# Token bases of the gate: whole tokens in pairs 3 to 6, or halves of the columns in pairs 3 to 7

## The chip, the cores and the metric

The kernel runs on one core of one Trainium2 chip, in one launch. The metric is the device time of that launch in microseconds (us). The core has a matrix engine (TensorE, PE in the profile; its weight loads are listed apart as PEld), VectorE (DVE), ScalarE (ACT), GpSimd (POOL) and SyncE (SP), which issues transfers. Each engine works through its own instructions in the order in which the built program lists them, and engines wait for each other through semaphores. Weights come from the device memory (HBM) by DMA into buffers in the on-chip memory (SBUF); matmul results land in PSUM buffers, which the program names by tags ("pt", "o", "dense", "s", two of each).

## The reference

Two transformer blocks follow each other on 512 tokens of width 1024. What concerns this change is the end of the second one: a mixture of 16 experts, each of which takes the 64 tokens with the highest affinity, and behind it a gate `g` that multiplies an embedding `e`:

```python
def expert_choice_ffn(h, w_router, w_gate, w_up, w_down):
    aff = jax.nn.softmax(jnp.einsum('bsd,de->bse', h, w_router).astype(jnp.float32), axis=-1)
    gates, idx = lax.top_k(aff.transpose(0, 2, 1), cap)          # cap = 64
    xe = h[bidx, idx]
    a = jnp.einsum('becd,edf->becf', xe, w_gate)
    b = jnp.einsum('becd,edf->becf', xe, w_up)
    ye = jnp.einsum('becf,efd->becd', jax.nn.silu(a) * b, w_down)
    return jnp.zeros_like(h).at[bidx, idx].add(ye * gates[..., None].astype(h.dtype))
...
x = x + expert_choice_ffn(rms_norm(x, norm_ffn[i]), w_router[i], w_gate[i], w_up[i], w_down[i])
g = jax.nn.sigmoid(rms_norm(x, norm_ple[i]) @ w_ple_gate[i])
e = rms_norm(p[i] @ w_ple_proj[i], norm_ple_post[i])
x = x + g * e
```

An expert has 2 x 1024 x 2048 weights in and 2048 x 1024 out, all fp32.

## The kernel before

**Pairs.** The 16 experts run as 8 pairs (`pr` 0 to 7): expert 2p sits in columns 0 to 63 of the array, expert 2p+1 in 64 to 127, so the two matmuls of a step run side by side. The weights of a pair are 48 chunks of 128 x 2048 fp32 (1.049 MB each, 50.3 MB a pair), two of them for each of 24 steps. `chunk` takes the next one and issues its transfer on SP's queue into the buffer that was used longest ago; that transfer waits until PE has read the buffer's former chunk. From pair 3 on (`RETIRE`) seven such buffers are left. A pair has four sections of four steps (`ga` is the gate projection, `ua` the up projection, two steps each; `sg` is their product on DVE, `pth` its transposes on PE, copied to `hts` by ACT), and then eight steps of the down projection `yd`, in two halves of the columns. Each half ends with `yg` and `ys` (the scaled result and its split in two parts), with its transposes `pty` copied to `yt`, and with a `spread`, which adds the rows into the token array `xt` (named `xk` in the profile): per group of 128 tokens two matmuls `po` and an addition on DVE.

**The gate.** Its product, (x after the mixture) times `w_ple_gate`, is linear before the normalisation, so it is built up while the experts run. `gate_base(t)` transposes what `xt` holds for token group t (eight transposes `ptg`, two ACT copies to the single buffer `xf`) and multiplies it by the gate's weights, both halves h of 512 columns (16 matmul instructions `pg` for each); `snap[t]` notes the pair in which that was. What later pairs add to these tokens goes another way: `gate_pair` multiplies the pair's own result by the gate's weights (`z`, 16 instructions for each half of the columns), splits it on ACT and DVE (`zs`), and scatters it (`po<-zs`, two matmuls and an addition, L1637) into the bases that exist already. Pair 7's `z` stays in PSUM and joins at the end.

**Order.** Such side work stands in the list `todo` as generators; `meanwhile(n)` takes n steps of them. `between` (L1651) is called after each of the 24 steps of a pair and takes `PACE[pr]` side steps on average; from pair 4 on (`HOLD`) their instructions stand behind the step's last expert matmul. `on_the_way` advances `route(pr + 1)` beside that: `bc` on PE, `ott`, `ix`, `at` on DVE, then the gather of the next pair's tokens `xg` by POOL's queue, and then an ACT instruction (L1485) that scales them.

Of the kernel before, what the change touches and what calls it, by code (L numbers as in the profile page):

```python
# [18 lines left out]
S = 512  # L19
# [8 lines left out]
XV = 4  # L28
ADA_N = 1
PO = 10  # L30
PACE = [1.0, 1.0, 1.0, 2.2, 2.2, 2.2, 2.2, 2.2]
ROUTE_PACE = 0.5
HOLD = 4
ADDPE = [1, 3, 5, 6]
TBK = 7
RETIRE = 3
BASE = {3: [0], 4: [1], 5: [2], 6: [3]}
E_AT = 1
ADA0 = 0
ADA_EVERY = 3  # L40
# [188 lines left out]
def _build(ctx, tc, nc, a, dbg, stop):  # L229
    V, A, T, P, SY = nc.vector, nc.scalar, nc.tensor, nc.gpsimd, nc.sync  # L230
# [25 lines left out]
    def ps(name, tag, bufs, shape=(128, 512)):  # L256
        tag = tag[1:] if tag[0] == "=" else TG[0].get(name, tag)
        return psp.tile(list(shape), FT, name=name, tag=tag, bufs=bufs)
# [25 lines left out]
    def t2k(name):  # L284
        return tmp[0].tile([128, S], FT, name=name, tag="t2k", bufs=nt2k[0])
# [23 lines left out]
    def weights(src, raw=None, p_=None, bufs=2):  # L309
        with tc.high_priority(offset=WO[0]):  # L310
            return weights_(src, raw, p_, bufs)
# [11 lines left out]
    def kview(w, k):  # L323
        return [t.rearrange("p (k c) -> p k c", k=k) for t in w]
# [764 lines left out]
    for j in range(22):  # L1089
        if j % 4 == 2 and j < 12:  # L1090
            nbs.append(na_bias(j // 4))
        wg = kview(weights(a["w_up"][2 * j]), 8)
# [6 lines left out]
        t = t2k("cv")  # L1099
# [13 lines left out]
    def g_split(kk):  # L1113
        g = [pb_.tile([128, S], FR, name="gh", tag="gh", bufs=2 * NT + 2) for _ in range(2)]
        split(gm[:, kk], g[0], g[1])
        return g

    for kk in range(22 - NT):
        w = weights(a["w_dn"][kk])
        g = g_split(kk)  # L1120
# [378 lines left out]
    todo = []  # L1499
# [21 lines left out]
    ple = {}  # L1521
# [27 lines left out]
    def halves(out, w, x_, start, stop):  # L1549

        for h in range(2):
            c_ = slice(64 * h, 64 * h + 64)
            T.matmul(out[c_], w[:, c_], x_, start=start, stop=stop)  # L1553
# [39 lines left out]
        for t in range(4):  # L1593
            V.scalar_tensor_tensor(e[t], e[t], re_[:, t:t + 1], gpost, op0=OP.mult, op1=OP.mult)

    def gate_base(t):

        xf = ple["xf"]
        for f in range(2):
            pt = ps("ptg", "pt", 2)  # L1600
            for k in range(4):
                c_ = 512 * f + 128 * k
                T.transpose(pt[:, 128 * k:128 * k + 128], xt[:, t, c_:c_ + 128], K["ident"])
            A.activation(xf[:, 4 * f:4 * f + 4], pt.rearrange("p (k c) -> p k c", k=4), AF.Copy)
        snap[t] = pairs[0]
        yield
        for h in range(2):
            pg = ps("pg", "o", 2)
            for k in range(8):
                halves(pg, xf[:, k], ple["wg"][k // 2][:, k % 2, S * h:S * h + S], k == 0, k == 7)  # L1610
                yield
            V.tensor_copy(ple["g"][t][:, S * h:S * h + S], pg)

    def gate_pair(pr, yts, ott, zl):

        zl += [ps("z", "o", 2) for _ in range(2)]
        at = [(n, y) for n, c in enumerate((4, 4) if pr < 7 else (4, 2, 2)) for y in range(c)]
        left = [list(range(8)), list(range(8))]
        while left[0] or left[1]:

            ready = [h for h in range(2) if left[h] and at[left[h][0]][0] < len(yts)]
            if ready:
                h = ready[0] if pr == 7 else max(ready, key=lambda h: (len(left[h]), -h))
                k = left[h].pop(0)
                halves(zl[h], yts[at[k][0]][:, at[k][1]], ple["wg"][k // 2][:, k % 2, S * h:S * h + S], k == 0, k == 7)
            whole[:] = [not l for l in left] if pr == 7 else whole
            yield
        if pr == 7:
            return
        zs = yy("zs")  # L1630
        for h in range(2):
            y = hl(zl[h], zs[:, h])
            yield
            for t in range(4):
                if snap.get(t, 8) <= pr:
                    g_ = ple["g"][t][:, S * h:S * h + S]
                    V.tensor_tensor(g_, g_, scatter(y, ott, t), op=OP.add)  # L1637
                    yield
# [9 lines left out]
    snap, pairs, whole = {}, [0], [False, False]  # L1648
    owed, way = [0.0], [0.0]

    def between(last):  # L1651

        owed[0] += PACE[pairs[0]]
        n = int(owed[0])
# [11 lines left out]
    for pr in range(8):  # L1666
        pairs[0] = pr
        if pr:
            while pr not in routed:
                on_the_way()  # L1670
        xe = routed[pr][0]
        if pr < 7:
            ways.append(route(pr + 1))
        if pr == RETIRE:
            ple_loads()
        if pr == E_AT:
            todo.append(embedding())
        todo += [gate_base(t) for t in BASE.get(pr, ())]
        hts, flip = None, []

        def turn():

            for sec, sg in flip:
                pt = ps("pth", "pt", 2)
                for f in range(4):
                    T.transpose(pt[:, 128 * f:128 * f + 128], sg[:, 128 * f:128 * f + 128], K["ident"])  # L1686
                A.activation(hts[:, 4 * sec:4 * sec + 4], pt.rearrange("p (f s) -> p f s", f=4), AF.Copy)  # L1687
            flip.clear()

        for sec in range(4):  # L1690
            acc_ = [ps("ga", "dense", 2), ps("ua", "s", 2)]
            for m in range(2):
                for kh in range(2):
                    wa, wb = chunk(4), chunk(4)
                    for k in range(4):
                        kk = 4 * kh + k
                        T.matmul(acc_[m][0:64], xe[:, kk, 0:64], wa[:, k], start=kk == 0, stop=kk == 7)  # L1697
                        mm = T.matmul(acc_[m][64:128], xe[:, kk, 64:128], wb[:, k], start=kk == 0, stop=kk == 7)  # L1698
                    if pr == 0 and sec == 0:
                        meanwhile(1)  # L1700
                    if m == 0 and kh == 0:
                        turn()
                    between(mm)
            if hts is None:
                hts = mp.tile([128, 16, 128], FT, name="hts", tag="hts", bufs=1)
            sg = s2k("sg")
            A.activation(sg, acc_[0], AF.Silu)  # L1707
            V.tensor_tensor(sg, sg, acc_[1], op=OP.mult)  # L1708
            flip.append((sec, sg))
        turn()  # L1710
        last = pr == 7
        if last:
            tc.keep_in_program_order(A.preload_act_table_set(LN_EXP))
        _, gs, ott = routed.pop(pr)
        ys, yts, z = yy("ys"), [], []
        if pr >= min(BASE):
            todo.append(gate_pair(pr, yts, ott, z))
        for q in range(2):
            parts = 2 if last and q else 1
            n = S // parts  # L1720
            for part in range(parts):
                yd = ps("yd", "s" if q > part else "dense", 2)[:, 0:n]
                for k in range(4 // parts):
                    wa, wb = chunk(4 * parts), chunk(4 * parts)
                    for k_ in range(4 * parts):
                        kk = 4 * parts * k + k_
                        T.matmul(yd[0:64], hts[:, kk, 0:64], wa[:, k_], start=kk == 0, stop=kk == 15)  # L1727
                        mm = T.matmul(yd[64:128], hts[:, kk, 64:128], wb[:, k_], start=kk == 0, stop=kk == 15)  # L1728
                    between(mm)
                yg = s2k("yg")[:, 0:n]  # L1730
                A.activation(yg, yd, AF.Copy, scale=gs)  # L1731
                y = hl(yg, ys[:, q, :, n * part:n * part + n])
                if pr >= min(BASE):
                    pt = ps("pty", "pt", 2)[:, 0:n]
                    for k in range(n // 128):
                        T.transpose(pt[:, 128 * k:128 * k + 128], yg[:, 128 * k:128 * k + 128], K["ident"])
                    yt = mp.tile([128, 4, 128], FT, name="yt", tag="yt", bufs=2)[:, 0:n // 128]
                    V.tensor_copy(yt, pt.rearrange("p (k c) -> p k c", c=128))  # L1738
                    yts.append(yt)
                while any(t not in snap for t in BASE.get(pr, ())):  # L1740
                    meanwhile()
                if not last:
                    todo.append(spread(y, ott, q))
                for t in range(4) if last else ():
                    x_ = xt[:, t, S * q + n * part:S * q + n * part + n]
                    V.tensor_tensor(x_, x_, scatter(y, ott, t), op=OP.add)
                    if last:
                        A.activation(s2k("sq")[:, 0:n], x_, AF.Square,
                                     accum_out=sx[:, 3 * t + q + part:3 * t + q + part + 1])
# [7 lines left out]
    for h in range(2):  # L1757
# [5 lines left out]
        for t in range(4):  # L1763
            c_, n = slice(S * h, S * h + S), 4 * h + t
            o = outs[:, S * t:S * t + S]
# [34 lines left out]
```

## Time and profile before

| | |
|---|---|
| median of 3 runs | 2080.02 us (2078.24 to 2080.1) |
| the profiled execution | 2082.14 us, of which its span is 2080.4 us |
| PE busy | 1946.9 us, 94% of the span |
| DVE, ACT, POOL busy | 770.2, 587.8, 126.8 us |
| moved by DMA | 523.2 MB, mean 251 GB/s |
| pairs 3 to 7, first expert matmul at | 1402, 1524, 1657, 1787, 1918 us; pair 7 ends at 2043 |

The mean over the span hides stages with different limits. The experts begin at 1030 us, and the stretches by pair, about 125 us each, are what this change touches. In the stretch of a pair the question is which of two is late at each step: the chunk (PE waits for DMA) or the buffer (SP waits for PE before it issues the next transfer).

### The profile page before, as it was taken

The numbers are of one execution on the slowest core, as the hardware profiler recorded it, in microseconds if no ns is written. First come the engines' busy times: TensorE is split into PE (matmuls) and PEld (weight loads), VectorE is DVE, ScalarE is ACT, GpSimd is POOL, SyncE is SP. The second block draws the span as 40 slices with busy tenths as digits, with TensorE's granted clock in tenths as the row PEclk, the third lists the DMA queues.
The fourth block names the chain that finished last, engine by engine and source line by source line (L and its number), as shares of the span: only waits on it lengthen the run. The fifth ranks groups of instructions, "written<-read, shape, count | busy, mean of one in ns | idle before, by whom it ended". The sixth has DMA issues, their size and how long they took to land.

```text
span 2080.4 us, 23393 instructions
## 1 busy us (share of the span) xinstructions
PE 1946.9 (94%) x9118; PEld 1088.8 (52%) x9118; DVE 770.2 (37%) x1665; ACT 587.8 (28%) x1138; POOL 126.8 (6%) x127
## 2 busy tenths in 40 slices
PE   7989999989999998999899978789799999999998
PEld 4667667768888887776533322223233333333333
DVE  4767767764444336675431111010011021110212
ACT  4755657643323234454111110000000000000013
POOL 1210201300100000001000000030000000000000
PEclk9999989989999999999899999999999999999999
DMA  7432313422322231224889899998999999999991
GB/s 306 122 127 73 101 51 122 143 87 100 122 93 100 97 126 50 78 77 165 327 370 419 355 421 419 420 410 360 421 393 378 394 412 378 400 391 385 398 420 48
DMA packets 94191, 523.20 MB, mean 251 GB/s; under 512 B 11405, under 2 KB 11829, under 8 KB 43136
## 3 DMA queue, kind: packets, MB, share of 16 engines
q1 hardware_dynamic: 88832, 500.47, 61.6%
q0 software_dynamic: 3904, 18.88, 2.4%
q10 hardware_dynamic: 1344, 2.35, 0.3%
q8 instruction: 72, 1.18, 0.2%
q14 instruction: 39, 0.32, 0.0%
HBM read 510.31 MB, written 4.27 MB: 247 GB/s over the span
## 4 chain that ended last, share of the span: by engine, by line
PE 75%; DMA 13%; DVE 6%; ACT 3%; issue 2%; POOL 1%; DVEq 0%; POOLq 0%; ACTq 0%; SPq 0%
PE ua L1697 6%; DMA ch<-in_w_ue_dram 6%; PE ga L1697 5%; PE ga L1698 5%; DMA ch<-in_w_de_dram 4%; PE yd L1727 4%; PE yd L1728 3%; PE z L1553 3%; PE pg L1553 2%; PE od L652 2%; PE ag L327 2%; PE ag L328 2%; PE ag L329 2%; PE av L327 2%; PE av L328 2%
## 5 line engine op out<-in xcount | busy, mean ns | idle before, releaser
L1698 PE MATMUL ua<-ch,xe 128*64 128x512 f32 x512 | 230.9, 595 | 17.3 <-DMA ch<-in_w_ue_dram 17.3
L1728 PE MATMUL yd<-ch,hts 128*64 128x512 f32 (+1 forms) x544 | 231.8, 572 | 16.0 <-DMA ch<-in_w_de_dram 16.0
L1697 PE MATMUL ga<-ch,xe 128*64 128x512 f32 x512 | 242.2, 609 | 0.0
L1698 PE MATMUL ga<-ch,xe 128*64 128x512 f32 x512 | 236.8, 607 | 5.0 <-DMA ch<-in_w_ge_dram 5.0
L1697 PE MATMUL ua<-ch,xe 128*64 128x512 f32 x512 | 232.8, 595 | 0.0
L1727 PE MATMUL yd<-ch,hts 128*64 128x512 f32 (+1 forms) x544 | 232.7, 572 | 0.0
L320 DVE TENSOR_TENSOR wlo<-pan,whi 128x1024 fp32r<-128x1024 f32 x119 | 147.8, 1242 | 160.9 <-ACT whi L317 158.7
L317 ACT ACTIVATE whi<-pan 128x1024 fp32r<-128x1024 f32 x119 | 125.8, 1057 | 201.1 <-PE ag L328 84.8
L1708 DVE TENSOR_TENSOR sg<-sg,ua 128x512 f32<-128x512 f32 x32 | 22.0, 686 | 264.6 <-PE ua L1698 264.6
L1728 PEld LDWEIGHTS yd<-ch,hts 128*64 128x64 f32 x544 | 72.0, 137 | 91.2 <-issue 59.1
L1697 PEld LDWEIGHTS ua<-ch,xe 128*64 128x64 f32 x512 | 67.3, 137 | 96.3 <-issue 94.4
L1698 PEld LDWEIGHTS ga<-ch,xe 128*64 128x64 f32 x512 | 66.7, 139 | 87.8 <-issue 77.3
L1727 PEld LDWEIGHTS yd<-ch,hts 128*64 128x64 f32 x544 | 71.3, 137 | 67.3 <-issue 65.7
L355 POOL TENSOR_TENSOR ada_a<-ada_a,adw 128x512 f32<-128x512 f32 x56 | 79.3, 1416 | 378.1 <-ACT ada_a L352 270.6
L1698 PEld LDWEIGHTS ua<-ch,xe 128*64 128x64 f32 x512 | 67.4, 137 | 63.4 <-issue 32.3
L333 DVE TENSOR_TENSOR ys<-yg,ys 128x512 fp32r<-128x512 f32 (+1 forms) x17 | 12.5, 736 | 235.9 <-ACT ys L332 235.9
L1697 PEld LDWEIGHTS ga<-ch,xe 128*64 128x64 f32 x512 | 66.3, 139 | 61.6 <-issue 60.9
L1687 ACT ACTIVATE hts<-pth 128x512 f32<-128x512 f32 x32 | 19.1, 596 | 265.1 <-PE pth L1686 265.1
L1731 ACT ACTIVATE yg<-yd,gs 128x512 f32<-128x512 f32 (+1 forms) x17 | 11.3, 662 | 291.1 <-PE yd L1728 220.2
L1553 PE MATMUL z<-ch,yt 128*64 128x512 f32 x320 | 89.0, 595 | 1.4 <-DVE yt L1738 1.3
L1707 ACT ACTIVATE sg<-ga 128x512 f32<-128x512 f32 x32 | 19.1, 597 | 224.5 <-PE ga L1698 204.2
L614 ACT ACTIVATE e<-e,m 128x256 f32<-128x256 f32 (+8 forms) x128 | 64.9, 508 | 29.1 <-DVE m L612 28.7
(902 smaller groups left out, 3732.9 us busy)
## 6 DMA issues: line engine op xcount, KB each, us to landing
ch<-in_w_de_dram SPq DMA_DIRECT2D x128, 1024.0 KB, 12.1
ch<-in_w_ue_dram SPq DMA_DIRECT2D x125, 1024.0 KB, 10.1
ch<-in_w_ge_dram SPq DMA_DIRECT2D x120, 1024.0 KB, 10.1
pan<-in_w_up_dram SPq DMA_DIRECT2D x44, 512.0 KB, 3.4
adw<-in_ada_dram SPq DMA_DIRECT2D x64, 256.0 KB, 2.7
pan<-in_w_in_dram SPq DMA_DIRECT2D x24, 512.0 KB, 3.9
pan<-in_w_dn_dram SPq DMA_DIRECT2D x22, 512.0 KB, 3.4
adr<-in_ada_dram SPq DMA_DIRECT2D x8, 1024.0 KB, 12.4
```

The lines of the kernel that those rows point to most:

```text
L317: A.activation(hi, raw, AF.Copy)
L320: eng.tensor_tensor(lo, raw, hi.bitcast(FT), op=OP.subtract)
L327: T.matmul(out, wh, xh, start=first, stop=False)
L328: T.matmul(out, wh, xl, start=False, stop=False)
L329: T.matmul(out, wl, xh, start=False, stop=last)
L355: P.tensor_tensor(ada_next[1], ada_next[1], w, op=OP.add)
L614: A.activation(e[:, :nk], e[:, :nk], AF.Exp, bias=m, scale=-1.0, accum_out=l)
L1553: T.matmul(out[c_], w[:, c_], x_, start=start, stop=stop)
L1697: T.matmul(acc_[m][0:64], xe[:, kk, 0:64], wa[:, k], start=kk == 0, stop=kk == 7)
L1698: mm = T.matmul(acc_[m][64:128], xe[:, kk, 64:128], wb[:, k], start=kk == 0, stop=kk == 7)
L1727: T.matmul(yd[0:64], hts[:, kk, 0:64], wa[:, k_], start=kk == 0, stop=kk == 15)
L1728: mm = T.matmul(yd[64:128], hts[:, kk, 64:128], wb[:, k_], start=kk == 0, stop=kk == 15)
```

## The change

`BASE` now lists pairs of token group and half of the columns. Pair 3 makes the bases of groups 0 and 1 for half 0, pair 4 those of groups 2 and 3 for half 0, pair 5 groups 0 and 1 for half 1, pair 6 group 2 and pair 7 group 3 for half 1. Each base transposes its token group anew. `gate_pair` makes and scatters `z` only for halves that have a base already, so pairs 3 and 4 make it for half 0 alone. `PACE` goes down in pairs 3 to 6.

```diff
-PACE = [1.0, 1.0, 1.0, 2.2, 2.2, 2.2, 2.2, 2.2]
+PACE = [1.0, 1.0, 1.0, 1.9, 1.9, 1.9, 2.1, 2.2]
...
-BASE = {3: [0], 4: [1], 5: [2], 6: [3]}
+
+BASE = {3: [(0, 0), (1, 0)], 4: [(2, 0), (3, 0)], 5: [(0, 1), (1, 1)], 6: [(2, 1)], 7: [(3, 1)]}
...
-    def gate_base(t):
+    def gate_base(t, h):
...
-        snap[t] = pairs[0]
-        yield
-        for h in range(2):
-            pg = ps("pg", "o", 2)
-            for k in range(8):
-                halves(pg, xf[:, k], ple["wg"][k // 2][:, k % 2, S * h:S * h + S], k == 0, k == 7)
-                yield
-            V.tensor_copy(ple["g"][t][:, S * h:S * h + S], pg)
+        snap[t, h] = pairs[0]
+        yield
+        pg = ps("pg", "o", 2)
+        for k in range(8):
+            halves(pg, xf[:, k], ple["wg"][k // 2][:, k % 2, S * h:S * h + S], k == 0, k == 7)
+            yield
+        V.tensor_copy(ple["g"][t][:, S * h:S * h + S], pg)
...
-        zl += [ps("z", "o", 2) for _ in range(2)]
+        hs = [h for h in range(2) if any(c[1] == h for p_, l in BASE.items() if p_ <= pr for c in l)]
+        zl += [ps("z", "o", 2) for _ in hs]
...
-        left = [list(range(8)), list(range(8))]
+        left = [list(range(8)) if h in hs else [] for h in range(2)]
...
-        for h in range(2):
+        for h in hs:
...
-                if snap.get(t, 8) <= pr:
+                if snap.get((t, h), 8) <= pr:
...
-        todo += [gate_base(t) for t in BASE.get(pr, ())]
+        todo += [gate_base(*c) for c in BASE.get(pr, ())]
```

The diff doesn't show what this moves. Line numbers are one higher behind the change. The built programs have the same instructions in the same order on POOL and SP; PE, DVE and ACT differ from pair 3 on. Instructions counted by pair, from the pair's first expert matmul to the next pair's (an instruction `z` or `pg` covers one half of the array, 64x512; `po` counts matmuls of scatters, 128x512):

| | z | pg | ptg | po |
|---|---|---|---|---|
| pair 3, before / after | 16 / 8 | 15 / 16 | 0 / 8 | 0 / 0 |
| pair 4 | 32 / 16 | 32 / 32 | 8 / 16 | 20 / 20 |
| pair 5 | 32 / 22 | 32 / 32 | 8 / 16 | 24 / 24 |
| pair 6 | 32 / 34 | 32 / 16 | 8 / 8 | 28 / 28 |
| pair 7, up to its first `po<-ys` of its own | 16 / 16 | 0 / 16 | 0 / 8 | 32 / 30 |

Three places, word for word. First ACT at the head of pair 4, before and after (`yg`, `ys`: the end of pair 3; `sg`: the first section; `xg`: the gathered tokens, which waits for the gather; `zs`: the split of pair 3's `z`; `hts`: the first section's transposes).

```order
L1731 ACTIVATE yg<-yd,gs 128x512
L332 ACTIVATE ys<-yg 128x512
L1707 ACTIVATE sg<-ga 128x512
L1485 ACTIVATE xg<-xg 128x1024
L332 ACTIVATE zs<-z 128x512 x2
L1687 ACTIVATE hts<-pth 128x512
```

```order
L1732 ACTIVATE yg<-yd,gs 128x512
L333 ACTIVATE ys<-yg 128x512
L1708 ACTIVATE sg<-ga 128x512
L333 ACTIVATE zs<-z 128x512
L1486 ACTIVATE xg<-xg 128x1024
L1688 ACTIVATE hts<-pth 128x512
```

In pair 4 one `zs` instead of two stands on ACT, and ahead of `xg` instead of behind it. In pairs 5 and 6 `zs` stays behind `xg`.

Second PE at the head of pair 5, from `bc` to the second section (expert matmuls left out; `po<-zs`: the scatter of pair 4's `z`), before and after.

```order
L1469 MATMUL bc<-slots,two 128x512
L1553 MATMUL z<-ch,yt 64x512 x6
...
L1553 MATMUL z<-ch,yt 64x512 x4
...
L1553 MATMUL z<-ch,yt 64x512 x2
...
L1686 MATMUL pth<-cst,sg 128x128 x4
...
L1537 MATMUL po<-zs,ott 128x512 x4
```

```order
L1470 MATMUL bc<-slots,two 128x512
L1554 MATMUL z<-ch,yt 64x512 x2
...
L1538 MATMUL po<-zs,ott 128x512 x4
...
L1687 MATMUL pth<-cst,sg 128x128 x4
...
L1538 MATMUL po<-zs,ott 128x512 x4
```

After the change there are two more `z` between the two steps of `ua` (a row like the one shown), 16 expert matmuls stand between `bc` and the first scatter, and that scatter stands ahead of `pth`; before, all scatters stood behind it.

Third DVE at the head of pair 6, from the index of the gather, before and after (L1637, L1638: the additions behind `po<-zs`).

```order
L1475 CAST at<-at 128x1
L333 TENSOR_TENSOR zs<-z,zs 128x512
L1708 TENSOR_TENSOR sg<-sg,ua 128x512
L333 TENSOR_TENSOR zs<-z,zs 128x512
L1637 TENSOR_TENSOR ch<-ch,po 128x512 x5
```

```order
L1476 CAST at<-at 128x1
L1709 TENSOR_TENSOR sg<-sg,ua 128x512
L334 TENSOR_TENSOR zs<-z,zs 128x512 x2
L1638 TENSOR_TENSOR ch<-ch,po 128x512 x4
L1709 TENSOR_TENSOR sg<-sg,ua 128x512
```

In pair 6 the product `sg` of the first section moves ahead of both `zs`; in pair 5 it stays behind the first.

## Rows read from the trace of the kernel before

**Rows 1.** The page: span, engines, 40 slices of 52 us
```profile
span 2080.4 us, 23393 instructions
...
PE 1946.9 (94%) x9118; PEld 1088.8 (52%) x9118; DVE 770.2 (37%) x1665; ACT 587.8 (28%) x1138; POOL 126.8 (6%) x127
...
DMA  7432313422322231224889899998999999999991
GB/s 306 122 127 73 101 51 122 143 87 100 122 93 100 97 126 50 78 77 165 327 370 419 355 421 419 420 410 360 421 393 378 394 412 378 400 391 385 398 420 48
```

**Rows 2.** Windows by pair: busy PE PEld DVE ACT POOL, clock, DMA, GB/s
```profile
1402.00:1525.00 123.00, 105.47 (x478) 36.69 (x474) 6.47 (x10) 6.67 (x11) 0.00 (x0) 0.99 0.95 388
1525.00:1657.00 132.00, 129.90 (x574) 45.82 (x575) 17.28 (x29) 11.09 (x19) 1.36 (x3) 0.99 0.97 385
1657.00:1787.00 130.00, 128.75 (x579) 44.41 (x576) 18.53 (x30) 10.56 (x18) 1.32 (x3) 1.00 0.99 399
1787.00:1918.00 131.00, 129.50 (x584) 46.10 (x584) 19.72 (x32) 10.72 (x18) 1.32 (x3) 1.00 0.98 390
1918.00:2043.00 125.00, 120.49 (x587) 47.24 (x587) 22.08 (x37) 14.75 (x33) 0.00 (x0) 1.00 0.89 362
```

**Rows 3.** Windows of 10 us, same columns: pair 3, then pair 7
```profile
1400.00:1410.00 10.00, 9.77 (x46) 3.65 (x45) 0.69 (x1) 0.00 (x0) 0.48 (x1) 1.00 0.38 144
...
1490.00:1500.00 10.00, 7.37 (x35) 2.29 (x32) 0.00 (x0) 0.00 (x0) 0.00 (x0) 1.00 1.01 420
1500.00:1510.00 10.00, 7.89 (x38) 2.63 (x36) 1.29 (x2) 1.32 (x2) 0.00 (x0) 1.00 1.02 423
...
2000.00:2010.00 10.00, 7.98 (x36) 2.31 (x32) 0.00 (x0) 0.00 (x0) 0.00 (x0) 1.00 1.02 422
2010.00:2020.00 10.00, 7.54 (x34) 3.07 (x32) 2.86 (x5) 2.39 (x5) 0.00 (x0) 1.00 1.01 418
```

**Rows 4.** Waits of PE, 1510 to 1918 us: total, times, longest
```profile
PE pth L1686 <- DVE sg L1708: 4.7, 3, 1.9
PE pty L1736 <- ACT yg L1731: 0.8, 1, 0.8
```

**Rows 5.** Waits of SP's queue in that stretch: the longest
```profile
SPq L1291 <- PE ua L1698: 105.3, 24, 5.8
```

**Rows 6.** Timeline of PE: start, length, then idle before in brackets
```profile
1540.86 1.89 PE L1553 MATMUL z<-ch,yt 128*64 128x512 f32 x8
...
1542.57 0.59 PE L1697 MATMUL ua<-ch,xe 128*64 128x512 f32 x1
...
1555.62 0.72 PE L1537 MATMUL po<-zs,ott 128*128 128x512 f32 x2
...
1584.54 1.09 PE L1603 MATMUL ptg<-cst,xk 128*128 128x128 f32 x8
1585.56 0.64 PE L1697 MATMUL ua<-ch,xe 128*64 128x512 f32 x1
1585.88 0.64 PE L1553 MATMUL pg<-ch 128*64 128x512 f32 x1
```

**Rows 7.** Timeline of all engines at the head of pair 5
```profile
1665.99 0.38 PE L1469 MATMUL bc<-slots,two 16*128 16x512 bf16 x1
...
1668.88 0.96 POOL L1477 DMA_INDIRECT xg<-xd,at  x1 [121.68 <-DVE at L1475]
...
1677.64 1.15 ACT L1485 ACTIVATE xg<-xg 128x1024 f32<-128x1024 f32 x1 [10.91 <-DMA xg<-xd,at]
...
1679.30 0.69 DVE L333 TENSOR_TENSOR zs<-z,zs 128x512 fp32r<-128x512 f32 x1 [11.21 <-ACT zs L332]
1679.91 0.68 DVE L1708 TENSOR_TENSOR sg<-sg,ua 128x512 f32<-128x512 f32 x1
...
1680.64 0.66 PE L1686 MATMUL pth<-cst,sg 128*128 128x128 f32 x4 [1.25 <-DVE sg L1708]
```

**Rows 8.** Window behind the longest of these waits, pair 4
```profile
1550.00:1553.00 3.00, 3.00 (x10) 1.16 (x11) 0.36 (x1) 0.60 (x1) 0.00 (x0) 0.50 0.99 418
```

More of the change, by code (lines that the diff above doesn't have):

```diff
@@ L1739, in _build @@
                     yts.append(yt)
-                while any(t not in snap for t in BASE.get(pr, ())):
+                while any(c not in snap for c in BASE.get(pr, ())):
                     meanwhile()
```

## The prediction

> **What bounds the kernel now.** I read the page first [rows 1]: PE is busy 94% of a span of 2080.4 us, but the two lines of slices beneath differ by stage. From the 20th slice on DMA moves some 400 GB/s, so a pair of experts can be limited by its weights or by PE's work, and the mean says nothing on which. The windows of 10 us settle it [rows 3]: at 1490 to 1510 DMA moves 420 to 423 GB/s while PE is busy 74 to 79%; there the transfers are the limit, and 420 is what they reach. A pair needs 50.3 MB, at 420 GB/s 119.8 us. The windows by pair show the other state [rows 2]: pairs 4, 5 and 6 take 132, 130 and 131 us at 385 to 399 GB/s with PE busy over 98%, 10 to 12 us more than the weights need. The list of PE's waits between 1510 and 1918 has no DMA in it, only 4.7 us for `sg` and 0.8 us for `yg` [rows 4], while SP's queue waits for PE to give buffers back [rows 5]. So in pairs 4 to 6 whatever PE does besides the experts is paid in full, down to 119.8 us a pair. Pair 3 is limited by DMA in its second half; so is the end of pair 7's stretch, where 2000 to 2020 shows 418 to 422 GB/s and PE busy 7.98 and 7.54 us of 10, a gap of 4.5 us in all [rows 3].
>
> **The change, part by part.** The counts by pair come from the order of the built programs, the prices from the timeline. Eight records of `z` (four instructions) occupy PE from 1540.86 until the next `ua` at 1542.57: 1.71 us, 0.43 us an instruction; `pg` has the same shape [rows 6]. Eight `ptg` run from 1584.54 to 1585.56, 1.0 us; a `po` pair is a record of 0.72 us, about 0.7 [rows 6].
>
> Pair 3. Before its first expert matmul nearly the same stands on PE (16 `pg` instead of 17). But the other half of the base used to sit between the first chunks, six instructions behind or inside each of the first two steps; now it sits in the third section. In 1400 to 1410 DMA moves only 144 GB/s, since all buffers are full and none has been read [rows 3]. The first buffers come back 6 x 0.43 = 2.6 us earlier, and the rest of the pair hangs on DMA. The moved half (16 x 0.43 = 6.9 us and 1.0 of transposes) lands where PE has a quarter of its time free [rows 3], which hides it; without that cover it would cost 7.9 us. Half of `z` falls away too, but near the pair's end, where DMA sets the pace: nothing. I take -2, since the moved half may hold up a chunk or two; bounds 0 (it eats all) and -6.2 (the whole of DMA's gap in that window, 0.62 of 10 us).
>
> Pair 4: 16 `z` fewer, 8 `ptg` more: -16 x 0.43 + 1.0 = -5.9. Its wait for `sg` goes as well. It is 1.9 us, the longest of the three [rows 4], and the 3 us behind it run at a granted clock of 0.50 [rows 8], that is at 1.2 instead of 2.4 GHz, which loses another 1.5. The cause shows in the same place of pair 5 [rows 7]: the gather of the next pair's tokens is issued at 1668.88 and lands at 1677.64; ACT stands at `xg` until then, `zs` is queued behind it, DVE stands at `zs`, `sg` behind that, and `pth` on PE waits 1.25 us. In pair 4 the new order has `zs` ahead of `xg` on ACT, so nothing on this chain waits for the gather; what is late next is `hts`, which only the down projection needs. -3.4, bounds 0 (another wait, below) and -3.4. Together -9.3.
>
> Pair 5: 10 `z` fewer, 8 `ptg` more: -10 x 0.43 + 1.0 = -3.3. Here `zs` stays behind `xg`, and the scatter of `zs` now stands on PE ahead of the second section. Before, DVE's first `zs` ended at 1679.30 + 0.69 = 1680.0, 14.0 us behind `bc` at 1665.99 [rows 7]. In the new order PE has only `bc` (0.4), four `z` (1.7) and 16 expert matmuls between `bc` and that scatter; the expert matmuls take 0.43 each as well, 6.8. It is there after 8.9 us and stands for 5.1. Behind it queue the second section's matmuls, and SP behind their buffers. The old wait of 1.25 goes. A halved clock behind it is likely, as in pair 4: 1.5 us. Net -3.3 + 5.1 - 1.25 + 1.5 = +2.0; bounds -1.5 (the gather lands 2 us sooner, no drop of the clock) and +4 (a drop twice as long, and half a microsecond more of waiting).
>
> The Trainium skill says in "TensorE: Matmul & The Clock Gate", part 1, that the halved clock is the array's resting state and that activity lifts it. By that rule the wait of pair 5 costs more than its own length. The trace agrees in pair 4, 0.50 behind 1.9 us of waiting [rows 8]; without the rule the sum would be 1.5 us lower.
>
> Pair 6: 16 `pg` fewer, 2 `z` more: -14 x 0.43 = -6.0. `sg` now stands ahead of `zs` on DVE, so the wait before `pth`, 1.5 us of the 4.7 (4.7 - 1.9 - 1.25), goes: -7.5, bounds -6 and -7.5.
>
> Pair 7: 16 `pg` and 8 `ptg` more, one `po` pair fewer: 6.9 + 1.0 - 0.7 = +7.2. The 4.5 us in which PE stood for DMA near the end can take part of it: PE comes later to those chunks, which then are there. +2.7, bounds +2.7 and +7.2. The order behind the last expert matmul is unchanged, so the tail stays.
>
> The new bases also add hand-offs from `ptg` over ACT to `pg`: one more each in pairs 4, 5 and 7. In the old one at 1584.54 a single `ua` instruction covers the copy, and `pg` starts at 1585.88 with no idle time before it [rows 6]. I take 0; without cover each could cost what the wait in pair 4 cost, 1.9 + 1.5 = 3.4, together 10.
>
> Sum: -2 - 9.3 + 2.0 - 7.5 + 2.7 = -14.1. Each pair stays above its 119.8 us: pair 4 goes from 132 to about 123, pair 6 from 131 to about 123.5. The profiled execution took 2082.14 us, of which its span is 2080.4; with the change I expect a span near 2066.3 and 2068 in all. The median of the runs is 2.1 us below the profiled one; taken from that median, the sum gives **2066.0**.
>
> **The rivals.** *The hand-offs and the clock eat more.* Each new base, and the scatter of pair 5, opens a gap on PE, and the clock halves behind each. For it: one wait of 1.9 us was enough for that [rows 8]. Against it: pair 5, with its wait of 1.25 us, has a mean clock of 1.00 [rows 2], and the copies have expert matmuls as cover in the order. Price: two or three of the three hand-offs at 3.4, +7 to +10: 2073 to 2076.
>
> *DMA is the limit already.* If 385 to 399 GB/s in pairs 4 to 6 were the most that DMA can move beside a busy PE, these pairs could not get shorter; pair 3's 2 us alone would be left: 2078 to 2080, no change that the measurement, good to about 0.2% or 4 us, can tell. For it: the DMA share there is 0.97 to 0.99 [rows 2]. Against it: no wait for DMA on PE, long waits of SP's queue for PE [rows 4, 5], and 418 to 423 GB/s in stretches where PE is held back [rows 3]. The Trainium skill, "DMA: Bandwidth & Descriptors", section Specifications, gives such a limit, about 358 GB/s of memory bandwidth for one core. By that rule the pairs were at their limit before, and the time would stay at 2080. The trace disagrees: 423 GB/s [rows 3].
>
> *Slower.* The wait of 5 us in pair 5 throws the clock down, and it stays at 1.2 GHz long behind it, since PE then works through its queue at half speed with waits between. Its place is the second section of pair 5. Half speed for 28 us would take back the 14 us; at 40 us the time would be 2066 + 20 - 1.5, some 2085. For it: the wait would be longer than any other in pairs 4 to 6. Against it: behind pair 4's wait the window shows 3 us at 0.50, and the mean over the pair is 0.99 [rows 2, 8].
>
> *Better than forecast.* The gather lands sooner, the clock holds, pair 3 gives up to 6 us: 2066 - 3.5 - 4, about 2058, to 2061.
>
> **How the numbers follow.** The forecast, 2061 to 2072, gets 0.62. Hand-offs and clock (2073 to 2076) 0.20, DMA as the limit (2078 to 2080) 0.09, slower 0.03, better 0.06. The range reaches over the better case and the hand-offs: 2059 to 2076, which leaves out about 0.14. Faster by over 0.2% is below 2075.9: the forecast, the better case and all but 0.01 of the hand-offs, 0.87. Within 0.2%: 0.10. Slower by over 0.2%: 0.03.
>
> **What would show it.** In the windows by pair: pair 4 near 123 us, pair 5 near 132 (130 before), pair 6 near 123.5, pair 7 near 128, at DMA rates up to 410 GB/s in pairs 4 and 6. In PE's waits: none for `sg` in pairs 4 and 6; a new one of about 5 us in pair 5, of the scatter `po` for `zs`, with a clock below 1 behind it. At 2000 to 2020 PE busy near 10 of 10. Records of `z` 256 instead of 320, `ptg` 64 instead of 32. The prediction is wrong if PE's new waits in pairs 4, 5 and 7 exceed 10 us, if DMA waits appear in pairs 4 to 6, or if those pairs keep their length with less on PE.

## The result and the profile after

The changed kernel takes 2064.78 us (median of 4 runs, 2063.72 to 2067.67), the kernel before 2080.06 beside it: a ratio of 0.9932, 95% interval 0.9919 to 0.9945, or 15.3 us. The profiled execution took 2067.67 us, the slowest of the four. Its page, beside [rows 1]:

```profile
span 2065.9 us, 23336 instructions
...
PE 1944.7 (94%) x9084; PEld 1090.8 (53%) x9084; DVE 769.5 (37%) x1662; ACT 591.2 (29%) x1144; POOL 126.8 (6%) x127
```

PE is busy only 2.2 us less than before, though the span is 14.5 us shorter. The windows by pair of the changed kernel, cut at each pair's first expert matmul (columns as in [rows 2]):

```profile
1400.50:1513.00 112.50, 101.35 (x470) 35.57 (x468) 6.81 (x10) 7.19 (x12) 0.00 (x0) 1.00 0.99 410
1513.00:1638.00 125.00, 124.10 (x551) 46.58 (x549) 16.80 (x28) 11.17 (x18) 1.36 (x3) 1.00 1.01 414
1638.00:1774.00 136.00, 131.08 (x575) 46.57 (x571) 18.56 (x30) 12.54 (x20) 1.32 (x3) 0.97 0.96 388
1774.00:1899.00 125.00, 125.00 (x555) 43.30 (x553) 18.76 (x31) 10.44 (x17) 1.32 (x3) 1.00 0.99 404
1899.00:2028.00 129.00, 128.23 (x620) 50.14 (x620) 22.27 (x37) 15.60 (x34) 0.00 (x0) 1.00 0.89 358
```

Pairs 3, 4 and 6 are shorter, pairs 5 and 7 longer. Pair 5 alone has a clock below 1, and its rate is 388 GB/s where it was 399. The lengths from one pair's first expert matmul to the next's, to a tenth (the tail runs from the start of the last `yd` to the end of the span; pair 4 of the kernel before begins at 1523.4, so that it is 133.9 us long and not the 132 of [rows 2]):

| | pair 3 | pair 4 | pair 5 | pair 6 | pair 7 | tail | sum |
|---|---|---|---|---|---|---|---|
| before | 121.1 | 133.9 | 130.2 | 130.9 | 124.0 | 38.1 | |
| after | 112.4 | 125.4 | 135.8 | 125.0 | 128.7 | 38.1 | |
| difference | -8.7 | -8.5 | +5.6 | -5.9 | +4.7 | 0 | -12.8 |
| predicted | -2 | -9.3 | +2.0 | -7.5 | +2.7 | 0 | -14.1 |

The 1.7 us that are missing to the 14.5 of the span lie ahead of pair 3. They are not the change's to claim: in two pairs of kernels below that are the same program up to there, pair 3 begins at 1400.5 and 1399.1, and at 1398.5 and 1396.6.

PE's waits from 1510 to 1910, where [rows 4] had three for `sg`:

```profile
PE po L1538 <- ACT zs L333: 4.1, 1, 4.1
PE pty L1737 <- ACT yg L1732: 1.6, 2, 0.8
```

The waits for `sg` are gone, and one of 4.1 us for `zs` has come; `pty` waits for `yg` once more than before. The place of the wait for `zs`, the head of pair 5 (the same instructions as in [rows 7]):

```profile
1649.45 0.39 PE L1470 MATMUL bc<-slots,two 16*128 16x512 bf16 x1
...
1652.33 0.96 POOL L1478 DMA_INDIRECT xg<-xd,at  x1 [115.14 <-DVE at L1476]
...
1661.03 1.15 ACT L1486 ACTIVATE xg<-xg 128x1024 f32<-128x1024 f32 x1 [10.88 <-DMA xg<-xd,at]
1662.09 0.58 ACT L333 ACTIVATE zs<-z 128x512 fp32r<-128x512 f32 x1
...
1662.72 2.37 PE L1538 MATMUL po<-zs,ott 128*128 128x512 f32 x4 [4.15 <-ACT zs L333]
```

ACT has nothing else to do; it stands at `xg` until the gather, issued at 1652.33, has landed. `zs` is queued behind it, and PE stands at the scatter for 4.15 us. What the clock does there, in windows of 3 us (columns as before; the third number from the right is the granted clock):

```profile
1659.00:1662.00 3.00, 0.00 (x0) 0.00 (x0) 0.00 (x0) 0.97 (x1) 0.36 (x2) 1.00 1.02 421
1662.00:1665.00 3.00, 2.28 (x4) 1.12 (x4) 1.97 (x3) 0.66 (x2) 0.00 (x0) 0.58 1.01 418
1665.00:1668.00 3.00, 3.00 (x9) 1.04 (x8) 0.69 (x1) 0.00 (x0) 0.00 (x0) 0.50 1.01 418
1668.00:1671.00 3.00, 3.00 (x13) 1.06 (x13) 0.00 (x0) 0.60 (x1) 0.00 (x0) 0.78 0.64 265
```

Behind the wait the clock is 0.58, 0.50 and 0.78 for 9 us. From 1659 DMA still moves 421 GB/s, from 1668 only 265, since the buffers are full and SP's queue waits up to 12.0 us for PE to read them: the pair loses its transfers' head start as well. The Trainium skill, "TensorE: Matmul & The Clock Gate", part 1, has the halved clock as the state of an idle array, which activity lifts. The last three of these windows agree with it; in the first PE does nothing and the clock is still 1.00, so the fall comes late.

The last group: windows of 10 us in pairs 3 and 7, beside [rows 3].

```profile
1400.00:1410.00 10.00, 10.00 (x50) 3.24 (x48) 0.69 (x1) 0.60 (x1) 0.00 (x0) 1.00 0.79 302
...
2000.00:2010.00 10.00, 9.23 (x55) 4.74 (x53) 3.95 (x6) 4.14 (x10) 0.00 (x0) 1.00 1.02 425
2010.00:2020.00 10.00, 10.00 (x67) 5.45 (x65) 2.33 (x6) 2.13 (x7) 0.00 (x0) 1.00 0.45 183
```

DMA's gap at the head of pair 3 has shrunk from 0.62 to 0.21 of 10 us, and PE's gaps near the end of pair 7 from 4.5 to 0.8 us.

### The profile page after: what moved, and what is told of

It is laid out like the page before. It is cut to its first block, busy times and chain, and to the rows that moved or that the text cites. A ratio compares the mean times of both kernels' runs of the same rounds, so it can differ in the third digit from the quotient of the medians.

```text
span 2065.9 us, 23336 instructions
## 1 busy us (share of the span) xinstructions
PE 1944.7 (94%) x9084; PEld 1090.8 (53%) x9084; DVE 769.5 (37%) x1662; ACT 591.2 (29%) x1144; POOL 126.8 (6%) x127
## 4 chain that ended last, share of the span: by engine, by line
PE 76%; DMA 13%; DVE 5%; ACT 3%; issue 2%; POOL 1%; DVEq 0%; POOLq 0%; SPq 0%; ACTq 0%
DMA ch<-in_w_ue_dram 6%; PE ua L1698 6%; PE ga L1699 5%; PE ga L1698 5%; PE yd L1729 4%; PE yd L1728 4%; DMA ch<-in_w_de_dram 4%; PE z L1554 3%; PE pg L1554 3%; PE od L653 2%; PE ua L1699 2%; PE po L1538 2%; PE ag L328 2%; PE ag L329 2%; PE ag L330 2%
## 5 line engine op out<-in xcount | busy, mean ns | idle before, releaser
L1554 PE MATMUL pg<-ch 128*64 128x512 f32 x256 | 76.8, 613 | 2.4 <-POOL ch L1566 2.4
L328 PE MATMUL ag<-hTh,whi 128*128 128x512 f32 x176 | 70.9, 403 | 2.2 <-ACT hTh L425 2.2
```

The source lines that it names most:

```text
L328: T.matmul(out, wh, xh, start=first, stop=False)
```

## The experiments

Each ratio is against runs of the kernel before beside it: 2080.06 us for the changed kernel, medians of 2078.95 to 2079.34 for the others. Kernels 7 and 10 leave out work, so part of their result is missing; they only serve to find out what a pair costs without it.

| kernel | us | ratio, 95% interval |
|---|---|---|
| changed kernel | 2064.8 | 0.9932 [0.9919, 0.9945] |
| 1 changed, `xg` behind `zs` | 2059.3 | 0.9909 [0.9893, 0.9925] |
| 2 before, `xg` behind `zs` | 2073.4 | 0.9968 [0.9959, 0.9977] |
| 3 changed, old pace | 2057.1 | 0.9896 [0.9881, 0.9911] |
| 4 as 3, `z` for both halves | 2075.6 | 0.9987 [0.9978, 0.9996] |
| 5 as 3, `xg` behind `zs` | 2057.7 | 0.9895 [0.9880, 0.9911] |
| 6 as 5, last base in pair 6 | 2060.7 | 0.9914 [0.9898, 0.9929] |
| 7 as 5, no `z` | 2072.4 | 0.9971 [0.9959, 0.9982] |
| 8 before, new pace | 2073.2 | 0.9973 [0.9963, 0.9984] |
| 9 before, half a base later | 2073.7 | 0.9976 [0.9966, 0.9985] |
| 10 as 7, `z`'s turns kept | 2051.7 | 0.9866 [0.9850, 0.9883] |

Their lengths by pair, from the traces (one execution each):

| | pair 3 | pair 4 | pair 5 | pair 6 | pair 7 |
|---|---|---|---|---|---|
| 1 | 112.4 | 125.4 | 128.9 | 125.0 | 128.7 |
| 2 | 121.7 | 130.3 | 128.9 | 129.3 | 124.0 |
| 3 | 114.4 | 123.7 | 129.7 | 125.9 | 127.8 |
| 4 | 116.7 | 135.5 | 132.0 | 124.8 | 127.5 |
| 5 | 112.5 | 124.5 | 131.1 | 125.3 | 127.5 |
| 6 | 112.4 | 123.9 | 129.7 | 130.8 | 123.9 |
| 7 | 112.9 | 131.4 | 131.0 | 129.0 | 128.0 |
| 8 | 121.7 | 128.5 | 125.4 | 131.0 | 126.6 |
| 9 | 116.1 | 134.5 | 130.1 | 131.0 | 124.0 |
| 10 | 112.3 | 123.8 | 125.2 | 121.7 | 130.4 |

### 1 and 2: the gather at the head of ACT's queue

```diff
-        A.activation(xg[:, 0:D], xg[:, 0:D], AF.Copy, scale=xg[:, D + 16:D + 17])
+        with ExitStack() as c_:
+            if zlast[0] is not None:
+                c_.enter_context(tc.issue_after(zlast[0].ins))
+            A.activation(xg[:, 0:D], xg[:, 0:D], AF.Copy, scale=xg[:, D + 16:D + 17])
...
-            y = hl(zl[h], zs[:, h])
+            y = zs[:, h]
+            zlast[0] = A.activation(y[:, 0], zl[h], AF.Copy)
+            V.tensor_tensor(y[:, 1], zl[h], y[:, 0].bitcast(FT), op=OP.subtract)
```

`zlast` is the ACT half of the last split of `zs`, which is written out here so that it can be named; nothing else changes. Expected of the changed kernel with this edit:

> The changed kernel, with ACT's scaling of the gathered tokens xg put behind the split zs of the pair before in every pair. Theory (the scatter in pair 5 waits for zs, which stands behind the gather): PE's wait of 4.15 us for zs in pair 5 goes, and with it the halved clock behind it, about 3 us; pair 5 goes from 136 to about 129 us and the time from 2064.8 to about 2058. Rival (that time is given back, since the weights in pairs 5 to 7 are late anyway): the wait goes, the time stays at 2063 to 2065, and waits for DMA appear instead.

and of the kernel before with it:

> The kernel before, with the same edit alone. Theory of the prediction (the waits for sg in pairs 4 to 6 of the kernel before come from the gather, which holds up zs and so sg): these waits, 4.7 us, go together with the halved clock behind the first, 2080 to about 2074. Rival (zs comes late because z itself ends late, just ahead of the second section, and sg stands behind zs on DVE): the waits shrink by no more than 1 us each, 2077 to 2080.

Measured 2059.3 and 2073.4. The head of pair 5 in the first, same instructions as above:

```profile
1650.85 0.96 POOL L1478 DMA_INDIRECT xg<-xd,at  x1 [115.25 <-DVE at L1476]
...
1653.71 0.60 ACT L1637 ACTIVATE zs<-z 128x512 fp32r<-128x512 f32 x1 [5.03 <-PE z L1557]
...
1657.02 1.20 PE L1541 MATMUL po<-zs,ott 128*128 128x512 f32 x4
...
1659.58 1.15 ACT L1489 ACTIVATE xg<-xg 128x1024 f32<-128x1024 f32 x1 [5.28 <-DMA xg<-xd,at]
```

The gather takes as long as ever, but `zs` no longer stands behind it and the scatter has no idle time before it. Only pair 5 differs from the changed kernel: 128.9 instead of 135.8, the full 6.9 us of wait and clock. In the kernel before, the three waits for `sg` vanish with the same edit, and pairs 4, 5 and 6 lose 3.6, 1.3 and 1.6 us. So the queue behind the gather is the cause in both kernels; the changed kernel escapes it in pairs 4 and 6 and meets it worse in pair 5.

### 3, 4 and 8: the pace, and the `z` that falls away

```diff
-PACE = [1.0, 1.0, 1.0, 1.9, 1.9, 1.9, 2.1, 2.2]
+PACE = [1.0, 1.0, 1.0, 2.2, 2.2, 2.2, 2.2, 2.2]
```

is kernel 3; kernel 4 has in addition `hs = [0, 1]` in `gate_pair`; kernel 8 is the kernel before with the new line.

> The changed kernel with the side steps of the kernel before (2.2 in pairs 3 to 7). Theory (work taken off PE is what counts, the pace matters only where it moves a scatter ahead of its zs): as fast as the changed kernel within 4 us, 2061 to 2069, with the wait for zs in another place (zs ahead of xg in pairs 4 and 5, behind it in pair 6). Rival (the pace carries the gain): 2072 to 2080.

> The kernel above (halves of the bases, side steps as before), but z is made and split for both halves of the columns in pairs 3 and 4, where half of it is used by nobody: 8 + 16 + 8 more z instructions at 0.43 us and two more splits. Theory: the 24 in the stretches that PE limits cost 10 us, the 8 of pair 3 some 2 to 3, so 11 to 14 us more than the kernel above. Rival (DMA sets the pace, so work of PE is hidden): within 3 us of it.

> The kernel before with the new pace only (1.9 in pairs 3 to 5, 2.1 in pair 6): nothing is saved, and up to 10 instructions of z slip from pairs 5 and 6 into later ones. If the gain comes from the halves and the z that falls away, this gives nothing: 2078 to 2086, and ACT still meets xg ahead of zs, so a wait behind the gather remains. Rival: the slower pace itself gives a part of the gain by spacing side work out; then 2066 to 2074.

Kernel 3 came out at 2057.1, lower than expected. The new pace doesn't carry the gain, it costs 7.7 us: with the old one `zs` stands ahead of `xg` on ACT in pairs 4 and 5, and pair 5 is 6.1 us shorter. (Its trace is of the slowest of its four executions, 2063.8 us: pair 3 begins at 1402.5, and is 114.4 us long where kernel 5, the same there, has 112.5.) Kernel 4 is 18.5 us slower than kernel 3, more than expected. By pairs that is 2.3, 11.8 and 2.3 us in pairs 3, 4 and 5, 15.0 over all five. In pair 4 only 7.8 of it is `z` itself; with the rest the wait for `sg` is back:

```profile
PE pth L1687 <- DVE sg L1709: 4.5, 3, 1.9
```

For two halves of `z` ACT again has `xg` first. Kernel 8 refutes my expectation of no gain: 5.7 us, as its rival had it. But its trace has another reason than spacing. Its list of waits has none of DVE's `sg` between 1495 and 1905, pairs 4 and 5 are 5.4 and 4.8 us shorter, and some of that is only put off: 20 more records of `z` stand in pair 7, which is 2.6 us longer. In its trace DVE makes the first section's `sg` ahead of both `zs` in pairs 4 to 6, where before it came behind the first of them ([rows 7] for pair 5). The same line of numbers thus takes a wait away in one kernel and makes one in the other.

### 9: half a base moved out of pair 3's head

```diff
-                halves(pg, xf[:, k], ple["wg"][k // 2][:, k % 2, S * h:S * h + S], k == 0, k == 7)
+                with ExitStack() as c_:
+                    if h and not t:
+                        c_.enter_context(tc.issue_after(mms[0].ins))
+                    halves(pg, xf[:, k], ple["wg"][k // 2][:, k % 2, S * h:S * h + S], k == 0, k == 7)
```

`mms[0]` is the last expert matmul of the step, set in `between`.

> The kernel before with one thing moved: the half of pair 3's base that stood between the first chunks (16 instructions pg) is held back to the second half of the up and third section's steps, as in the changed kernel. Nothing is saved. Theory: DMA's idle time at 1400 to 1410 shrinks from 0.62 to about 0.25 of 10 us, pair 3's chunks land 4 to 6 us earlier, the moved work hides, and pairs 4 to 7, which are set by PE, carry the gain to the end: pair 3 at 115 to 117 us, the time 2073 to 2076. Rival, the prediction's value: 2 us, 2077 to 2078; then most of pair 3's shortening in the changed kernel comes from its z that falls away.

Measured 2073.7, as the theory had it: 5.5 us for an edit that saves no work. Pair 3 is 5.0 us shorter, pairs 4 to 7 are as before within 0.6, and the first window of pair 3 is

```profile
1400.00:1410.00 10.00, 10.00 (x48) 3.23 (x46) 0.00 (x0) 0.60 (x1) 0.00 (x0) 1.00 0.73 279
```

DMA moves 279 instead of 144 GB/s there [rows 3]. The moved half costs nothing where it now stands, among PE's waits for chunks.

### 5 and 6: the old pace and `xg` behind `zs`; pair 7's base in pair 6

Kernel 5 has both edits above; kernel 6 in addition:

```diff
-BASE = {3: [(0, 0), (1, 0)], 4: [(2, 0), (3, 0)], 5: [(0, 1), (1, 1)], 6: [(2, 1)], 7: [(3, 1)]}
+BASE = {3: [(0, 0), (1, 0)], 4: [(2, 0), (3, 0)], 5: [(0, 1), (1, 1)], 6: [(2, 1), (3, 1)]}
```

> The changed kernel with the old pace and with the scaling of xg held behind zs on ACT. With the old pace alone 2057.1 us were measured, and one wait for sg of 1.6 us was left in pair 6, where xg still stands ahead of zs. If the gather at the head of ACT's queue is the cause, that wait goes and with it up to 1.5 us of low clock: 2054 to 2056, pair 6 at 123 to 124.5 instead of 125.9. Rival: pair 6 is at its transfers already, or something else delays sg; then 2057 again, with a wait for sg still in pair 6.

> The same kernel with the last base, group 3 of half 1, made in pair 6 instead of pair 7. My theory: pair 7 pays only a part of the 7.2 us of that base, since PE stands for transfers near its end anyway, while pair 6 pays all of 7.9. So pair 6 +6 to +8, pair 7 -3.5 to -5, in all +2 to +4: 2057 to 2060. Rival: pair 7 pays in full (or its low clock does); then the two cancel and the time stays within 1 us of the kernel with the base in pair 7.

Kernel 5 measured 2057.7, no better than kernel 3 at 2057.1. Its wait for `sg` in pair 6 is gone, but pair 6 is only 0.6 us shorter. Expected were 2054 to 2056; the rival's 2057 held, and though no wait for `sg` is left, its first form, pair 6 at its transfers, shows. PE's weight loads (PEld) wait there for chunks, 1.8 us in kernel 3 and more in kernel 5 (1766.5 to 1891.8 us):

```profile
PEld yd L1734 <- DMA ch<-in_w_de_dram: 3.1, 4, 1.7
```

Its pair 5 is 1.4 us longer than kernel 3's, but kernel 6, the same program up to there, has 129.7 again: so much can differ from one execution to the next. The weight loads' waits for chunks differ with it, 2.1 us there in kernel 5 and 0.8 in kernel 6. Kernel 6 measured 2060.7, by the medians 3.1 us slower, as expected; but the two intervals overlap, and in the traces pairs 6 and 7 together are only 1.9 us longer. Pairs 6 and 7 of kernel 5,

```profile
1766.50:1891.80 125.30, 123.70 (x552) 43.90 (x551) 19.29 (x31) 10.67 (x18) 1.32 (x3) 1.00 1.00 403
1891.80:2019.30 127.50, 126.74 (x618) 49.78 (x619) 22.17 (x37) 15.42 (x34) 0.00 (x0) 1.00 0.90 365
```

and of kernel 6:

```profile
1762.60:1893.50 130.90, 130.90 (x593) 48.35 (x591) 19.90 (x32) 11.76 (x20) 1.32 (x3) 1.00 0.99 396
1893.50:2017.30 123.80, 119.42 (x579) 46.74 (x580) 22.09 (x37) 14.21 (x31) 0.00 (x0) 1.00 0.90 365
```

The same base costs 5.5 us in pair 6 and 3.6 in pair 7, where without it PE's busy time falls by 7.3 but its idle time grows from 0.8 to 4.4: pair 7 covers about half.

### 7 and 10: the floor of a pair, and what a base at the head costs

```diff
-        hs = [h for h in range(2) if any(c[1] == h for p_, l in BASE.items() if p_ <= pr for c in l)]
+        hs = [0, 1] if pr == 7 else []
```

> The same kernel with z left out in pairs 3 to 6, and with it the split and the scatters of z into the bases (what these pairs add to the bases is left out of the result). This asks for the floor of a pair. If it is set by its 50.3 MB at 420 GB/s, pairs 4 to 6 fall to 119.8 to 121 us each at 415 to 421 GB/s, and PE's waits there become waits for DMA; the time is 2033 to 2040. Rival: DMA beside a busy PE can move no more than the 410 to 414 GB/s of the changed kernel's pairs 3 and 4; then 122 to 123 us a pair and about 2042 to 2045. Second rival: something else sets the length, and the pairs stay over 124, the time over 2048.

Measured 2072.4, 15 us slower than with `z`. Of the three only the second rival's open end, over 2048, holds it, and what sets the length there was in none. Without `z` the bases slide to the heads of the pairs, and there they meet the gather. From the waits of PE between 1495 and 1905 and the head of pair 4:

```profile
PE pg L1557 <- ACT ch L1608: 19.3, 3, 7.1
```

```profile
1527.22 1.00 POOL L1478 DMA_INDIRECT xg<-xd,at  x1 [129.97 <-DVE two L1468]
...
1529.09 1.10 PE L1607 MATMUL ptg<-cst,xk 128*128 128x128 f32 x8
...
1535.82 1.15 ACT L1489 ACTIVATE xg<-xg 128x1024 f32<-128x1024 f32 x1 [12.24 <-DMA xg<-xd,at]
1536.88 1.06 ACT L1608 ACTIVATE ch<-ptg 128x512 f32<-128x512 f32 x2
...
1537.51 1.98 PE L1557 MATMUL pg<-ch 128*64 128x512 f32 x4 [6.32 <-ACT ch L1608]
```

The copies of the transposed tokens (`ch<-ptg`) stand in ACT's queue behind `xg`, and PE waits 6.3 us for them. This is the hand-off of the prediction's rival, which the changed kernel doesn't show: its bases stand in the middle of the pairs. Kernel 10 puts them back there by keeping the empty turns of `gate_pair` (all of its `yield`, none of its matmuls).

> The kernel with z left out of pairs 3 to 6 once more (with its split and scatters, so that part of the result is missing), but with the empty turns kept, so that the bases stay in the middle of the pairs instead of sliding to their heads behind the gather on ACT. If that slide cost the former its 15 us, pairs 4 to 6 now come to 119.8 to 122 us each at 410 to 420 GB/s with waits for DMA on PE, and pair 7 to 121 to 125: in all 2033 to 2042. Rival: the pairs have a floor of 124 to 125 us from something else; then 2045 to 2052.

Measured 2051.7: 20.7 us less than kernel 7, some 7 for each of the three waits. The rate and PE in pairs 4 to 6, and PE's waits from 1495 to 1905:

```profile
1512.40:1636.20 123.80, 116.35 (x517) 42.71 (x516) 14.69 (x25) 10.62 (x17) 1.36 (x3) 1.00 1.00 411
1636.20:1761.40 125.20, 117.41 (x515) 42.46 (x513) 14.75 (x24) 10.72 (x17) 1.32 (x3) 1.00 1.00 408
1761.40:1883.10 121.70, 109.56 (x475) 39.98 (x474) 14.06 (x23) 9.53 (x15) 1.32 (x3) 1.00 1.01 416
```

```profile
PE yd L1730 <- DMA ch<-in_w_de_dram: 14.0, 11, 2.3
PE ga L1700 <- DMA ch<-in_w_ge_dram: 9.4, 8, 1.4
PE ua L1700 <- DMA ch<-in_w_ue_dram: 9.4, 7, 1.4
```

Now PE waits 32.8 us for chunks. All of `z` in pairs 3 to 6 is gone, and the time falls by only 6 us against kernel 5: over most of these pairs DMA is the limit. The 119.8 us was not reached; pairs 4 to 6 average 123.6 at 408 to 416 GB/s, and the time is in the rival's range, 2045 to 2052. But 123.6 is no floor of the transfers alone, since PE still holds them up in the middle of a pair:

```profile
1592.00:1602.00 10.00, 10.00 (x50) 3.42 (x48) 0.23 (x1) 0.00 (x0) 0.00 (x0) 1.00 0.92 371
1602.00:1612.00 10.00, 10.00 (x50) 3.37 (x48) 1.14 (x2) 0.60 (x1) 0.00 (x0) 1.00 0.96 367
```

So pair 4 of the changed kernel, at 414 GB/s, is within 2 us of what it takes without `z`, and most of what `z` still costs is covered. Where the floor of a pair lies with its bases spread better, no run shows.

## Why the prediction was right, and where not

2066.0 was forecast, 2064.8 measured, and the mechanisms were the ones named: less on PE in pairs 4 and 6, no wait for `sg` there, a new wait for `zs` in pair 5 with a low clock, a part of pair 7's base hidden. But that the sum is so close is luck, since two errors cancel. Pair 3 gave 6.7 us more than its term, pairs 4 to 7 gave 8.0 less (-4.1 instead of -12.1).

To see where, I added up the intervals from each PE record to the next by the tile of the former. "Expert" contains `ga`, `ua`, `yd` and the waits behind them:

| after minus before | expert | `z` | `pg` | `ptg` |
|---|---|---|---|---|
| pair 3 | 102.9 to 95.1 | -3.4 | +1.1 | +1.4 |
| pair 4 | 92.4 to 91.1 | -7.8 | +0.2 | +1.0 |
| pair 5 | 88.5 to 94.9 | -5.1 | +1.1 | +0.9 |
| pair 6 | 89.0 to 88.3 | +1.7 | -7.0 | 0 |
| pair 7 | 93.6 to 89.7 | 0 | +7.8 | +1.1 |

**Pair 3, -2, measured -8.7.** Two steps failed. "I take -2" for the moved half: kernel 9 shows 5.0 us in the pair and 5.5 in the time. The bound of -6.2, DMA's gap in the first window, was the better reading; the fear that the moved half would hold up chunks had no row. And "near the pair's end, where DMA sets the pace: nothing" for `z`: the windows that I cited stop at 1510, where DMA did set the pace. In the ten microseconds behind them, which the prediction did not look at, it no longer does:

```profile
1510.00:1520.00 10.00, 10.00 (x50) 3.38 (x48) 0.00 (x0) 0.00 (x0) 0.00 (x0) 1.00 1.01 419
```

PE is busy all of it. The `z` of the pair's end stand there, and 3.4 us of them were saved in full: the changed kernel's pair 3 is 3.7 us shorter than that of kernel 9, which has all of them.

**Pair 4, -9.3, measured -8.5.** `z` gave 0.9 more than its 6.9. Expert fell by 1.3 instead of the 3.4 for wait and clock. The 3.4 was right: in kernel 2, which takes the wait away alone, expert is 89.1. But in the changed kernel it is 91.1, with no idle interval of PE to show for it. The list of the weight loads' waits (PEld) in pair 4, 1513 to 1638 us, has the reason, which the prediction put at nothing: chunks that come late.

```profile
PEld ua L1699 <- DMA ch<-in_w_ue_dram: 1.1, 2, 0.6
PEld ga L1699 <- DMA ch<-in_w_ge_dram: 0.6, 2, 0.3
```

In pair 4 of kernel 2, and in pairs 4 to 6 of the kernel before, that list has no wait for a chunk. PE's own list can't show these, because the pair's first expert keeps PE busy while the second waits:

```profile
1545.54 1.07 PE L1698 MATMUL ua<-ch,xe 128*64 128x512 f32 x2
1546.30 0.13 PEld L1699 LDWEIGHTS ua<-ch,xe 128*64 128x64 f32 x1 [0.57 <-DMA ch<-in_w_ue_dram]
1546.30 0.64 PE L1699 MATMUL ua<-ch,xe 128*64 128x512 f32 x1
...
1549.88 0.74 PE L1538 MATMUL po<-ys,ott 128*128 128x512 f32 x2
```

The second expert starts 0.76 us behind the first, and `po` behind both comes 4.3 us after the step's start instead of 3.6 as in kernel 2; the next step of `ua` does the same. So pair 4 is at its transfers for part of its length. No run takes these waits away alone; that they make the 2 us is read from the trace.

**Pair 5, +2.0, measured +5.6.** Wait and clock were right: 5.1 + 1.5 = 6.6 predicted, 6.9 by kernel 1, with a shorter wait (4.15) and a longer drop of the clock. The work was not: -3.3 - 1.25 = -4.6 predicted, -1.3 measured (kernel 1 against before, 128.9 and 130.2). `z` and `ptg` gave -5.1 and +0.9, as they should, but `pg` took 1.1 more for the same instructions, and expert 1.2 more in kernel 1 (89.7 against 88.5), although its wait had gone. Of that, 0.8 is a wait at the head of the pair that wasn't there before and that the prediction did not have:

```profile
1640.14 0.65 PE L1737 MATMUL pty<-cst,yg 128*128 128x128 f32 x4 [0.77 <-ACT yg L1732]
```

Why `pg` and the rest got slower stays open.

**Pair 6, -7.5, measured -5.9.** The wait for `sg` is gone. Two more `z` instructions cost 1.7 instead of 0.9, and of the wait's 1.5 us only 0.7 is seen in expert.

**Pair 7, +2.7, measured +4.7.** The base cost 7.8 + 1.1 on PE instead of 6.9 + 1.0; expert gave 3.9 back of the 4.5 expected. The value lies inside the bounds of 2.7 and 7.2.

**Hand-offs and tail, 0 and 0.** Both right, by the list of waits and the 38.1 us of the tail. Kernel 7 shows that the bound of 3.4 us for each was too low where the copy stands behind the gather, some 7. Of the signs against the forecast, one is near: PE's own list has no wait for DMA in pairs 4 to 6, but that of the weight loads has 1.7 us in pair 4.

The rival by which DMA was the limit before is refuted by the pairs that got shorter, at 410 and 414 GB/s where there had been 388 and 385. The Trainium skill's figure of about 358 GB/s for one core ("DMA: Bandwidth & Descriptors", Specifications) is exceeded over the whole of these pairs. In a weaker form the rival was near: pair 4 already waits for chunks, and kernel 10, mostly at that limit, is only 6 us below kernel 5. The slower rival's drop of the clock lasted 9 us, not 28.

**The versions that beat both.** Kernels 1, 3 and 5 take 2059.3, 2057.1 and 2057.7 us, 5 to 8 us less than the changed kernel; the intervals of 3 and 5 don't touch its own. Which of the three is fastest can't be told from these runs.

## What to carry to other kernels

An in-order queue makes a short instruction as late as the longest wait ahead of it: before moving side work, list for each engine which instruction in front waits for a transfer, and put what PE needs ahead of it; here one such edit was worth about 6 us in either kernel. Where two matmuls share the array, read the waits of the weight loads too, since one half at work hides the other's wait. Read windows up to the very boundary of a stage before calling work there hidden, since the limit can change from transfers to compute in its last 14 us. A sum that comes out right is no proof of its terms: compare each stage's length, and test the pace and the work apart, since a tuned number that helps one order can hurt another.

## What the runs showed of the hardware

- A wait of 4.15 us on PE left the granted clock at 0.58, 0.50 and 0.78 over the next 9 us; with the wait it cost 6.9 us. In the kernel before, 1.9 us of waiting was followed by 0.50 [rows 8].
- The indirect gather of the tokens took 8.7 us from its issue to the scaling that waited for it (1652.33 to 1661.03), 8.8 in the kernel before [rows 7] and 8.6 at the head of pair 4 in kernel 7.
- Two matmuls of 64 columns run side by side in the array, and when the weight load of one half waited 0.57 us for its chunk, that half stayed behind to the end of the step: 4.3 us instead of 3.6, with no idle time on PE (pair 4 of the changed kernel and of kernel 2).
